# A hybrid attention and gating layer on eight cores: ordering by a build-time list scheduler, weights in column blocks, a lagging out-projection

## Chip, cores, metric

One Trainium2 chip, all 8 cores, each with one of the eight sequences of the batch and its own copy of the weights; nothing passes between cores. The metric is the device time of the slowest core in microseconds (us).

The program has a second, slower state: in some executions the cores of one die show a lower granted TensorE clock and take longer. Such runs are marked slow, and all ratios below are of fast runs only.

Names: PE is TensorE, DVE VectorE, ACT ScalarE, POOL GpSimd, SP the engine that issues most DMAs. SBUF is the memory in which the kernel keeps its tiles; its matmuls write to PSUM, here eight banks of 512 columns, which ScalarE or VectorE instructions then empty. A supertile is 512 rows of x (four tiles of 128); a sequence has eight.

In the profile lines, xn is the scaled x, xT its transpose, PT the exponentials of the scores, LR the attention gate over the softmax denominator, mixT the input of the out-projection, vln the layer norm of v_s and st_lr its scale, xe the copy of x for the residual, and pb or pp a PSUM bank.

## The reference, cut to what matters

```python
h = rmsnorm(x, norm_g)                                   # x: (8, 4096, 1024) float32
q, k, v, z_a, u, v_s, z_s = split(h @ w_in + b_in)       # 512,128,128,512,512,512,512 columns
attn = banded_sink_attention(q, k, v, sinks) * silu(z_a) # window 128, 8 heads of 64, 2 kv heads
u, v_s = gelu(u), gelu(v_s)
sgu = u * (tril(W_s) @ layernorm(v_s) + b_s) * silu(z_s) # in chunks of 128 positions
x = x + concat(attn, sgu) @ w_out + b_out                # residual, and a bias
return rmsnorm(x, final_norm_g)
```

## The kernel before: the parts that matter

Every engine runs a fixed list of instructions; semaphores are derived from declared reads and writes. PSUM banks are given out in rotation, whether the next one is free or not:

```python
def newbank():
    b = bank_ctr[0] % NB          # NB = 8
    bank_ctr[0] += 1
    return b
```

The weights arrive as three column ranges of eight row blocks, so the first projection needs all eight blocks of its range. The q and k groups are emptied by VectorE, and one set of two groups is issued as one piece of work:

```python
PIECES = [(0, 768), (768, 1792), (1792, 2816)]
# ... in fm_unit, after 8 matmuls for each group:
if func == AF.Identity:           # q and k
    S.op("dve", lambda e, ...: e.tensor_scalar(out=dst, in0=pbank[b][:], scalar1=bias_fm[:, fi:fi + 1], ...))
else:                             # gelu and silu groups
    S.op("act", lambda e, ...: e.activation(out=dst, in_=pbank[b][:], func=func, bias=...))
```

The bias b_out is added to x on GpSimd, at a fixed place in its list, before the residual needs it; x stays in SBUF from load to residual:

```python
def XB_units(st):                 # one per tile
    S.op("pool", lambda e: e.tensor_tensor(out=xs, in0=xs, in1=bout[:], op=ALU.add), ...)
```

The order of one supertile is written by hand (C1: scores, exp, masks; C2: values and denominators; Eu: out-projection of the same supertile; f: one projection piece of the next):

```python
f(1); C1_unit(st, 0)(); f(1); C1_unit(st, 1)(); C2_unit(st, 0)(); f(1)
C1_unit(st, 2)(); C2_unit(st, 1)(); Eu[0]()
f(1); C1_unit(st, 3)(); C2_unit(st, 2)(); Eu[1]()
f(1); C2_unit(st, 3)(); Eu[2](); f(100); Eu[3]()
# ... then XB_units, gelu groups, v_s, silu groups, mixing of the next supertile
```

The softmax here doesn't subtract the row's maximum and nothing guards it: scores larger than these inputs give would overflow.

## Time and profile before

| | before |
|---|---|
| times known at the prediction | 642.26, 643.53, 693.18 us |
| span of the profiled run, clock of its cores | 628.8 us, 0.949 to 0.959 |
| first attention scores | 89.3 us (the prediction reads 88.3) |
| seven periods from there | 492.0 us, 70.3 each |
| rest | 47.5 us |

A period here is the time from the first scores of one supertile to those of the next.

### The profile page before, as it was taken

To read this page: it belongs to the slowest core of one execution; us is meant where nothing else is said; L and a number is where in the kernel's file an instruction comes from. 1 tells how busy PE (TensorE), PEld (TensorE's weight loads), DVE (VectorE), ACT (ScalarE), POOL (GpSimd) and SP (SyncE) were. 2 spreads that over 40 slices of the span, in tenths; PEclk is the share of its full clock that TensorE was granted. 3 is DMA by queue.
4 is the path that set the end of the run, shared out by engine and by line. 5 is a ranking of instruction groups with operands and counts; after the bars stand their busy time and mean duration, and the time that the engine had idled before them with its cause. 6 is when DMAs were issued, how large, how long until landed. Compare 5 with 4: busy or idle time off the path is not lost.

```text
span 628.8 us, 9475 instructions; the slowest of 8 cores (623.3 to 628.8 us)
## 1 busy us (share of the span) xinstructions
PE 533.3 (85%) x3042; PEld 240.1 (38%) x3042; DVE 300.5 (48%) x510; ACT 346.6 (55%) x691; POOL 269.9 (43%) x286
## 2 busy tenths in 40 slices
PE   1569479899889998899889989899889989999673
PEld 1234233354434453344334443444335443444121
DVE  1230384445554464545545454545545454555244
ACT  4003573546853596557743695448734695443742
POOL 0464593274435353365336253456327253443310
PEclk9979787899999999999989999999989999999688
DMA  8999900240013200330013100340014100110002
GB/s 226 274 321 317 144 2 1 101 167 2 0 68 108 95 1 0 135 135 0 2 68 133 68 1 11 124 135 1 1 68 160 42 2 1 68 67 1 1 35 100
DMA packets 15747, 50.08 MB, mean 80 GB/s; under 512 B 2513, under 2 KB 2769, under 8 KB 15698
## 3 DMA queue, kind: packets, MB, share of 16 engines
q1 hardware_dynamic: 14546, 47.38, 22.5%
q0 software_dynamic: 1152, 2.10, 2.4%
q8 instruction: 25, 0.41, 0.3%
q14 instruction: 24, 0.20, 0.1%
HBM read 34.79 MB, written 16.78 MB: 82 GB/s over the span
## 4 chain that ended last, share of the span: by engine, by line
PE 49%; ACT 14%; issue 12%; DVE 9%; POOL 7%; DMA 7%; SPq 1%; POOLq 0%; DVEq 0%; ACTq 0%
PE pb L373 24%; PE pb L570 14%; DMA y_t<-w_in 7%; PE pb L422 5%; ACT PT L469 4%; DVE y_t L578 2%; ACT junk L584 2%; PE pb L401 2%; ACT LR L511 2%; POOL LR L516 2%; DVE st_bn L428 2%; POOL st_rs L314 2%; POOL st_lr L432 2%; PE pb L496 1%; DVE PT L478 1%
## 5 line engine op out<-in xcount | busy, mean ns | idle before, releaser
L373 PE MATMUL pb<-xT,w_in_bf 128*128 128x512 bf16 x1088 | 250.6, 388 | 11.8 <-POOL w_in_bf L266 8.5
L373 PEld LDWEIGHTS pb<-xT,w_in_bf 128*128 128x128 bf16 x1088 | 106.6, 100 | 147.5 <-issue 29.7
L570 PE MATMUL pb<-w_out_bf,mixT 128*128 128x512 bf16 x512 | 126.8, 405 | 22.2 <-DVE qT L379 16.5
L584 ACT ACTIVATE junk<-y_t 128x1024 bf16<-128x1024 f32 x32 | 33.8, 1057 | 124.4 <-DVE y_t L578 124.4
L474 POOL TENSOR_SCALAR_AFFINE_SELECT PT<-PT 128x512 bf16<-128x512 bf16 x62 | 42.6, 710 | 106.2 <-ACT PT L469 106.0
L570 PEld LDWEIGHTS pb<-w_out_bf,mixT 128*128 128x128 bf16 x512 | 50.6, 103 | 95.0 <-issue 48.4
L337 POOL TENSOR_TENSOR x_t<-x_t,bout_sb 128x1024 f32<-128x1024 f32 x32 | 82.4, 2607 | 0.0
L516 POOL TENSOR_TENSOR LR<-LR,zaT 128x512 f32<-128x512 f32 x32 | 36.9, 1154 | 105.8 <-ACT LR L515 105.8
L469 ACT ACTIVATE PT<-pb 128x512 bf16<-128x512 f32 x126 | 64.0, 606 | 18.7 <-PE pb L461 18.6
L422 PE MATMUL pb<-w_in_bf,xT 128*128 128x512 bf16 x256 | 60.7, 380 | 0.0
L432 POOL TENSOR_TENSOR st_lr<-st_ve,neghalf 128x1 f32<-128x1 f32 x32 | 17.6, 551 | 88.5 <-DVE st_ve L430 88.5
L593 DVE SCALAR_TENSOR_TENSOR y_t<-y_t,st_fr,gf_sb 128x1024 f32<-128x1024 f32 x32 | 44.6, 1394 | 23.0 <-ACT st_fr L591 23.0
L520 DVE TENSOR_TENSOR mixT<-pb,LR 128x512 bf16<-128x512 f32 x32 | 22.1, 692 | 67.9 <-POOL LR L516 64.9
L578 DVE TENSOR_TENSOR y_t<-pb,x_t 128x512 f32<-128x512 f32 x64 | 41.0, 681 | 15.3 <-PE pb L570 15.3
L426 ACT ACTIVATE vs_f<-pb 128x512 f32<-128x512 f32 x32 | 19.1, 597 | 52.2 <-PE pb L424 26.1
L478 DVE TENSOR_TENSOR PT<-PT,mask_sb 128x512 bf16<-128x512 bf16 x64 | 30.7, 514 | 25.8 <-ACT PT L469 25.8
L543 POOL TENSOR_TENSOR gate<-uT,zsT 128x512 bf16<-128x512 bf16 x32 | 39.6, 1268 | 1.8 <-ACT zsT L383 1.8
L428 DVE BATCH_NORM_STATS2 st_bn<-vs_f 128x6 f32<-128x512 f32 x32 | 22.0, 688 | 36.4 <-ACT vs_f L426 36.4
L511 ACT ACTIVATE LR<-pb,esink_col 128x128 f32<-128x128 f32 x128 | 37.1, 389 | 3.2 <-PE pb L501 3.2
L434 DVE TENSOR_SCALAR vln<-vs_f,st_mv,st_lr 128x512 bf16<-128x512 f32 x32 | 17.5, 546 | 37.4 <-POOL st_lr L432 37.4
L305 ACT ACTIVATE junk<-x_t 128x1024 bf16<-128x1024 f32 x32 | 33.7, 1054 | 1.9
L496 PE MATMUL pb<-PT,v_r 128*64 128x512 bf16 x126 | 20.9, 407 | 16.2 <-DVE PT L478 13.4
(59 smaller groups left out, 536.4 us busy)
## 6 DMA issues: line engine op xcount, KB each, us to landing
x_t<-x SPq DMA_DIRECT2D x32, 512.0 KB, 4.0
out<-y_t SPq DMA_DIRECT2D x32, 512.0 KB, 2.8
x_t<-w_in SPq DMA_DIRECT2D x10, 512.0 KB, 9.0
y_t<-w_in SPq DMA_DIRECT2D x6, 512.0 KB, 10.1
x_t<-w_in SPq DMA_DIRECT2D x6, 384.0 KB, 9.2
w_out_bf<-w_out POOLq DMA_DIRECT2D x8, 256.0 KB, 9.3
y_t<-w_in SPq DMA_DIRECT2D x2, 384.0 KB, 11.5
sgt<-sgu_wT SPq DMA_DIRECT2D x1, 512.0 KB, 7.1
```

Source lines behind the costliest of these rows:

```text
L337: S.op("pool", lambda e: e.tensor_tensor(out=xs, in0=xs, in1=bout[:], op=ALU.add), reads=[("x", slot), "c_bout"], writes=[("x", slot)])
L373: ins = e.matmul(pbank[b][:], lhsT=w_in[:, k, col:col + 128], rhs=xT[:, k, :], start=(k == 0), stop=(k == 7))
L422: e.matmul(pbank[b][:], lhsT=xT[:, k, tt * 128:(tt + 1) * 128], rhs=w_in[:, k, OFF_VS:OFF_VS + 512], start=(k == 0), stop=False)
L469: S.op("act", lambda e, g=g, kb=kb, b=b: e.activation(out=PT[:, pp, kb, g, :], in_=pbank[b][:], func=AF.Exp, scale=0.125), reads=[("pb", b ...
L474: return e.affine_select(out=v, in_=v, pattern=[[0, 4], [-1, 128]], compare_op=ALU.is_ge, fill=0.0, base=-1, channel_multiplier=1)
L511: ins = e.activation(out=LR[:, lb, c * 128:(c + 1) * 128], in_=pbank[bd_][:, c * 128:(c + 1) * 128], func=AF.Ln, bias=esink_col[:, c:c + 1])
L516: S.op("pool", lambda e: e.tensor_tensor(out=LR[:, lb, :].rearrange("p (c q) -> p c q", c=4), in0=LR[:, lb, :].rearrange("p (c q) -> p c q ...
L543: S.op("pool", lambda e, jj=jj, gb=gb: e.tensor_tensor(out=gate[:, gb, :], in0=uT[:, jj, :], in1=zsT[:, jj, :], op=ALU.mult), reads=[("uT" ...
L570: ins = e.matmul(pbank[banks[hf]][:], lhsT=mixT[:, ec, tt * 128:(tt + 1) * 128], rhs=w_out[:, ec, hf * 512:(hf + 1) * 512], start=(ec == 0 ...
L578: ins = e.tensor_tensor(out=y_t[:, ys, hf * 512:(hf + 1) * 512], in0=pbank[banks[hf]][:], in1=x_t[:, slot, hf * 512:(hf + 1) * 512], op=AL ...
L584: S.op("act", lambda e: e.activation(out=junk[:], in_=y_t[:, ys, :], func=AF.Square, accum_out=st_fs[:, ys:ys + 1]), reads=[("y", ys)], wr ...
L593: S.op("dve", lambda e: e.scalar_tensor_tensor(out=y_t[:, ys, :], in0=y_t[:, ys, :], scalar=st_fr[:, ys:ys + 1], in1=gf[:], op0=ALU.mult, ...
```

## The change

The hand-written order is replaced by a graph of operations with estimated costs and a list scheduler that runs at build time. At each step it takes the operation that can start first on any engine, and it gives a PSUM bank to whatever starts next. Some operations may go to either of two engines. Otherwise:

- weights in 22 column blocks of 128 (each enough for one group of eight matmuls);
- the out-projection of a supertile is offered one supertile later (the lag), so it can fill TensorE during attention;
- x is loaded a second time for the residual, and GpSimd adds b_out to this copy;
- one exp and one mask over two banks (1024 columns), and powers on GpSimd in place of small Ln and Exp.

The diff has 1,400 lines; its core is this (cuts marked):

```diff
-def newbank(): ... rotation ...
-run(A_pre_units(0)) ... f(1); C1_unit(st, 0)(); ...          # order by hand
+class Scheduler:                                             # cut to the choice
+    while done < len(ops):
+        for e in ENGS:
+            for o in avail[e]:
+                est = max(free[e], o.nready)                 # and the earliest free bank
+                # skip if another allowed engine would finish earlier by estimate
+                key = (est, o.prio, o.n)
+        ... take the best, free[e] = est + cost ...
+# weights
+def load_w(cb): G.op("sp", dma w_in[cb] ...); G.op({"dve": (1.22, fn), "pool": (2.6, fn)}, ...)
+# either engine
+G.op({"act": (1.16, fa), "dve": (0.85, fd)}, ...)            # xn: scaling of x
+G.op({"dve": (0.68, copy), "act": (1.06, copy)}, ...)        # xT out of PSUM
+G.op({"dve": (0.745, ...), "act": (0.69, ...)}, ...)         # q, k out of PSUM
+G.op({"dve": (0.75, mul), "pool": (1.25, aff)}, ...)         # mask of 1024 columns
+# second read of x, bias
+def load_xe(n):
+    G.op("sp", dma xe <- x[n] ...)
+    G.op("pool", lambda e: e.tensor_tensor(out=xe[:, s, :], in0=xe[:, s, :], in1=bout[:], op=ALU.add), cost=2.6, ...)
+# lag: out_tile(4 * (st - 1) + tt) is offered together with attention(st, j)
```

## The prediction

> **What bounds the kernel now.** I looked first at the cores and the granted clock, then at the page's busy line and 40 slices, then at the order of TensorE's work in one supertile of 512 rows, its waits, and the chain that ended last. From the page of the kernel before:
>
> ```profile
> PE 533.3 (85%) x3042; PEld 240.1 (38%) x3042; DVE 300.5 (48%) x510; ACT 346.6 (55%) x691; POOL 269.9 (43%) x286
> ...
> PE   1569479899889998899889989899889989999673
> ...
> PEclk9979787899999999999989999999989999999688
> DMA  8999900240013200330013100340014100110002
> GB/s 226 274 321 317 144 2 1 101 167 2 0 68 108 95 1 0 135 135 0 2 68 133 68 1 11 124 135 1 1 68 160 42 2 1 68 67 1 1 35 100
> ```
>
> TensorE is the only engine near its limit, and not everywhere: slices 0 to 4 (0 to 79 us) are a start-up in which the DMA is full and TensorE is not; then comes a plateau; the last two slices fall off. The timeline gives the boundaries. The first attention scores start near 88.3 us, the same point of the eighth supertile is at 581.3 us, so seven periods take 493.0 us (70.4 each); the last attention and out-projection take 47.5 us more.
>
> How short could a period be? I take start-to-start times from the timeline at full clock: 32 projection matmuls 6.90 us (0.216 each), 16 of the out-projection 3.46, the four v_s tiles 8.59, the V block 1.79, 16 transposes 0.99, four scores 0.54, one attention tile's eight value and denominator matmuls 0.98, the mixing 1.0. A supertile has 136, 64, 1, 1, 32, 16, 4 tiles and 1 of these: 29.3 + 13.8 + 8.6 + 1.8 + 2.0 + 2.1 + 3.9 + 1.0 = **62.5 us**, so 8 x 62.5 = 500 us for the program. The span of 628.8 us has 129 us in which the array does not stream at full rate. TensorE's waits between 131 and 551 us (six periods) show why:
>
> ```profile
> PE pb L570 <- DVE qT L379: 14.0, 11, 2.3
> PE pb L461 <- ACT PT L469: 8.6, 6, 1.4
> PE pb L496 <- DVE PT L478: 6.1, 6, 1.0
> PE pb L373 <- ACT zsT L383: 2.2, 6, 0.4
> ```
>
> They sum to some 32 us with the small ones, 5.3 per period. The out-projection does not need qT: it waits for the bank that the fixed rotation gives it, until VectorE, behind other work in its fixed order, has emptied a q projection from it. The timeline shows that such a pause costs twice:
>
> ```profile
> 322.69 0.60 PE L501 MATMUL pb<-PT,ones 128*64 128x512 bf16 x4
> 325.29 5.30 PE L570 MATMUL pb<-w_out_bf,mixT 128*128 128x512 bf16 x16 [2.00 <-DVE qT L379]
> ...
> 338.49 3.62 PE L570 MATMUL pb<-w_out_bf,mixT 128*128 128x512 bf16 x16
> ```
>
> After 2.00 us of idleness the same 16 matmuls take 1.7 us longer; in that stretch the granted clock is 0.77, 0.50, then 0.70. This happens in every second period (70.7 against 69.0 us).
>
> **What the Trainium skill says.** "TensorE: Matmul & The Clock Gate", Part 1: an idle array falls to half clock and needs a few us of work to return; the window is free-running. The trace agrees (0.50 above), and shows that a 2.0 us pause can be enough. The same part says that dense matmuls on three or more cores of a die take it to a 13/16 clock. This profile does not show that: the seven periods ran at 0.98. Of the three times, 693.18 us may be such a state, but has no trace. "PSUM — Partial Sum Buffer", Specifications: eight banks, and GpSimdE reads none of them; in the trace every pb tile is read by ACT or DVE, so only they can empty banks for the new scheduler. "DMA: Bandwidth & Descriptors", Queues, rings and completion order: each DMA engine takes turns between the rows that have work. So w_out on GpSimd's queue will share the engines with weights still in flight on SyncE's. Before it ran after them (144 GB/s in slice 4, engines full), so no row shows the sharing yet.
>
> **The change, part by part.** The matmuls are the same, 3042 on both sides, so 500 us remains the floor for TensorE; what can shrink is the 129 us beside it.
>
> Steady state. Banks go to whichever group is next instead of in rotation; q, k, xn and xT may be emptied by ACT or DVE (in the built order 20 of 40 q and k groups and 9 of 32 transposes go to ACT); the out-projection of the supertile before fills TensorE while attention waits for ACT. In the built order the attention phase has out groups between scores and values. Other engines per period: exp over two banks instead of one (63 instead of 126 of 606 ns) and no tiny Ln and Exp of the final norm (64 of 204 ns) relieve ACT, which takes some q and xT copies instead; it stays near the 43.5 us it has now. DVE gets 57 double masks (at most 2 x 514 ns) for 64 single ones, gives up 12 q and k groups (745 ns), 9 xT copies (683), and takes 19 more x scalings (852): near 38 against 36. GpSimd loses 56 of 62 masks (710 ns) and gains 32 pairs of small operations (190 + 551 ns) for the final norm: 82.4 + 39.6 + 36.9 us of unchanged rows and about 75 us of small ones, 29 per period. All are far below 62.5. I leave 2 us per period for waits and changes of array tiling, no re-warming: 64.5 against 70.4, times seven: **-41 us**.
>
> Start. Before: 88.3 us until the first scores. After: weights come in column blocks, and each of 22 blocks lets one group of eight matmuls run, so TensorE follows the DMA. What must land before the V block, last in the order, on SyncE's queue: 4 tiles of x, 22 blocks, two late constants, 4 tiles of the next x, 3 of the one after (the built order puts these between the blocks), 35 x 0.524 = 18.3 MB, with 1.2 MB of constants on ACT's queue. Slices 0 to 3 delivered 3.55 MB by 15.7 us, then about 0.318 MB per us. Block 15 (26 transfers, 14.8 MB with constants) lands near 53 us, the V block (19.6 MB) near 66 us. But w_out is released block by block from block 14 on; alone it took 2.1 MB at about 0.135 MB per us, about 2 us each; six of them before the V block push it to **about 78 us**. By then TensorE has done two sets of transposes, twelve u and gate groups, v_s, mixing, five q and k groups, two of the next supertile and a few scores: 47 us. Left: 500 - 47 = 453. Before, at 88.3 us, some 44 were done and 455 left. So the start gains about **-10 us**: much less than "weights arrive by column" promises, as the same bytes must come and more x is put before them.
>
> End. Before: 47.5 us for 19.7 us of matmuls. After, the out-projections of the last two supertiles (27.6 us) and attention (6 us) are left together; they cover the last softmax chain, perhaps 4 us of gaps remain, and about 8.5 us after the last matmul (residual, square, power, scale, store) are as before. **-15 us**.
>
> x twice. 16.8 MB more reads: at plateau the DMA share is 0.16 and 56 GB/s flow; one period's 4 more tiles (2.1 MB) take 7 us of DMA in 64. Hidden.
>
> Sum: 79.5 (V block landed, converted, copied) + 453 + 7 x 2 + 4 + 8.5 = 559 us of span. Before, the median of 643.53 is 14.7 above the profile's span; added: **573 us**. By differences: 643.5 - 41 - 10 - 15 = 577; I choose 571 between them and a slightly luckier DMA order.
>
> **Rivals.** (1) A new wait replaces the old: the order on every engine is fixed at build time from estimated costs, and a strict order of gelu, silu and exp phases on ACT forbids matmuls of a later phase. If semaphore delays, or ACT in the attention phase (four tiles of 2 x 1.04 + 1.17 + 0.63 us plus eight squares of 1.25: 26 us beside 32 us of matmuls), slip, 4 to 5 us per period stay, and the time is 590 to 600. For it: ACT is tight there. Against: the costs in the source (0.69, 1.25, 2.6, 1.73 us) match the trace's rows (691, 1054 + 189, 2607, 8 x 216 ns). (2) The start stays DMA-bound: w_out and early x push the V block to 85 us: 580. If the engines overlap both queues better than I assume, it lands at 68: 561. (3) The denser array trips the 13/16 clock in every run: 500/0.8125 = 615 us of matmuls, about 660 to 670 in all, slower. Against: the plateau is 92% busy now without it. Chance 3%.
>
> **Range and chances.** The start varies by 10 us either way, the bubbles by 10, the end by 3: low 549, high 593. Faster by over 2% is below 630.7 us, which only rival 3 or a badly wrong order misses.
>
> **What would show it.** Right: TensorE at 9 from slice 6 to nearly the end, periods of 64 to 65 us, no wait on a bank above 5 us in total, clock near 0.99 after the start, DMA at 9 until about 80 us, HBM reads of about 51 MB. Wrong: exp or a mask as TensorE's largest wait on the plateau (rival 1), projections waiting for weights beyond 80 us (rival 2), clock near 0.81 on all cores (rival 3).

## More of the kernel before

The prediction shows the page, the waits and the timeline. What it did not look at closely is the following view, the groups of instructions of VectorE and GpSimd by shape. After the count come the busy time in us and the mean of one in ns, then the idle time before the group and who ended it.

```profile
L478 DVE TENSOR_TENSOR PT<-PT,mask_sb 128x512 bf16<-128x512 bf16 x64 | 30.7, 514 | 25.8 <-ACT PT L469 25.8
...
L434 DVE TENSOR_SCALAR vln<-vs_f,st_mv,st_lr 128x512 bf16<-128x512 f32 x32 | 17.5, 546 | 37.4 <-POOL st_lr L432 37.4
```

The first is a mask on the exponentials, the second the output of the layer norm of v_s (vln); both are means over the whole run. The prediction took such means for fixed costs. The layer norm comes close to one (544 to 548 ns), the mask does not: half of them take 426 ns or less, the longest 2559.

## The result, and the profile after

| | before | after |
|---|---|---|
| median, all runs of the comparison | 642.89 us (4 runs) | 592.67 us (4 runs, all fast) |
| fastest run | 630.42 us | 591.43 us |
| ratio of fast runs | | 0.9404 (0.9373 to 0.9435) |

A ratio is the mean time of one kernel's fast runs over that of the other's of the same rounds, so it is not quite the ratio of the medians quoted. The gain looks larger in the medians because the three times known before were all slow runs: the fourth took 630.42 us, and in later rounds the fast runs of the kernel before lay between 625.75 and 630.71. In the terms of those rounds (about 628 us) the changed kernel takes **590.6 us**; the runs below are compared with that. As the ratio rests on one fast run of the kernel before, its interval is 2 us either way, and every gain below carries that. The kernel is 6% faster, and 21.7 us slower than predicted.

The mean granted clock of a die rose. Before:

```profile
die 0 (median of its cores): 623.7 us, clock 0.953
```

After:

```profile
die 0 (median of its cores): 587.4 us, clock 0.984
```

Most of this lies at the two ends (0.89 to 0.96 until the first scores, 0.76 to 0.93 from the last supertile's first scores on, on the profiled core); in the six periods between, it rose from 0.99 to 1.00, as the half-clock stretches are gone.

The page of the changed kernel, to be read against the page in the prediction:

```profile
PE 523.7 (89%) x3042; PEld 233.3 (39%) x3042; DVE 346.1 (59%) x438; ACT 331.0 (56%) x566; POOL 251.4 (43%) x277
...
PE   0688696999999899999899889999999889989971
...
PEclk9999988999999899999999999999999999999997
DMA  8999980510135312132213105230421013200342
...
HBM read 51.57 MB, written 16.78 MB: 116 GB/s over the span
```

TensorE is at 9 or near it from slice 7 on, but there are 8s on the whole plateau: this is where the time is missing. TensorE's waits for a named releaser (us in all, times, longest) show what took the place of the waits before:

```profile
PE pp L481 <- DVE xn L467: 14.6, 4, 12.2
PE pp L577 <- DVE vln L552: 8.0, 5, 2.7
PE pp L497 <- DVE w_fm L447: 7.5, 4, 4.7
PE pp L634 <- DVE mixT L657: 4.2, 4, 1.7
PE pp L681 <- DVE mixT L657: 3.7, 3, 1.8
PE pp L634 <- DVE v_r L526: 3.4, 1, 3.4
```

The first and third belong to the start. The others are waits for VectorE, of two kinds. L577 waits for the layer norm, its input. L634 has PT and v_r as inputs, not mixT: where it waits for mixT, it waits for a PSUM bank that VectorE has yet to empty. With the smaller waits of that kind (L681 for xe and xT, L481 for xT, L497 for xe) some 8 us of bank waits are left after the first scores. I add up the timeline of TensorE from first scores to first scores, and subtract from each period its number of matmuls at full-clock durations. This gives the loss of each period:

| part of the span (us) | predicted | measured |
|---|---|---|
| until the first scores | 79.5 | 81.25 |
| matmuls at full rate after that | 453 | 452.6 |
| losses in eight supertiles | 7 x 2 + 4 = 18 | 8.6, 8.2, 2.2, 7.4, 3.8, 5.0, 5.2, 4.6 = **45.0** |
| after the last matmul | 8.5 | 12.5 |
| span | 559 | 591.3 |

The split between the second and third row depends a little on the durations that are called full-clock (with those of the prediction it is 455.5 and 42.1); differences between runs of the same order do not. So the losses are what went wrong. Why is VectorE late? Its groups by shape, changed kernel:

```profile
L625 DVE TENSOR_TENSOR PT<-PT,mask_sb 128x1024 bf16<-128x1024 bf16 x57 | 57.0, 1012 | 5.5 <-ACT PT L612 4.7
...
L686 DVE TENSOR_TENSOR xe<-pp,xe 128x512 f32<-128x512 f32 x64 | 43.6, 686 | 55.3 <-PE pp L681 48.6 <-POOL xe L667 6.5
L552 DVE TENSOR_SCALAR vln<-vs_f,st_mv,st_lr 128x512 bf16<-128x512 f32 x32 | 27.4, 857 | 22.9 <-POOL st_lr L550 22.4
...
L467 DVE TENSOR_SCALAR xn<-xa,st_rs 128x1024 bf16<-128x1024 f32 x23 | 20.8, 918 | 16.9 <-POOL st_rs L461 11.9 <-PE pp L481 4.9
```

The layer-norm output has the same shape as before and takes 857 ns instead of 546. The residual (L686), which reads PSUM, takes 686 ns where it took 681. A mean hides how this comes about. Here is the timeline of VectorE in one stretch, then that of GpSimd (start, duration, instruction):

```profile
230.97 1.60 DVE L625 TENSOR_TENSOR PT<-PT,mask_sb 128x1024 bf16<-128x1024 bf16 x1
232.49 0.74 DVE L503 TENSOR_SCALAR qT<-pp,bias_fm_sb 128x512 bf16<-128x512 f32 x1
233.15 0.68 DVE L657 TENSOR_TENSOR mixT<-pp,LR 128x512 bf16<-128x512 f32 x1
233.75 1.57 DVE L625 TENSOR_TENSOR PT<-PT,mask_sb 128x1024 bf16<-128x1024 bf16 x1
```

```profile
230.87 1.16 POOL L653 TENSOR_TENSOR LR<-LR,zaT 128x512 f32<-128x512 f32 x1 [4.60 <-ACT LR L651]
231.98 2.80 POOL L667 TENSOR_TENSOR xe<-xe,bout_sb 128x1024 f32<-128x1024 f32 x1
```

A mask with GpSimd idle takes 0.68 or 0.69 us (33 of 33 in this run). The first mask here begins 0.10 us after GpSimd's LR product, which ends at 232.03, and ends at 232.57, 0.54 us later: it stood still until GpSimd was done. Now the bias addition, which was issued while the mask worked, takes 2.80 us instead of 2.35: it stood still in turn. The q and mixT instructions, which read PSUM, run beside it in 0.74 and 0.68 us, undisturbed. The second mask begins at 233.75 inside the bias addition and ends at 235.32, 0.54 us after the addition (234.78). So it is in the whole run: 18 masks began inside an LR product or a bias addition, and each ended 0.55 us after it.

The Trainium skill describes this: "SBUF — State Buffer", section "SBUF: two separate sides", says that VectorE and GpSimd share a pair of SBUF ports under an exclusive lock, which GpSimd contends for with VectorE instructions in a two-port mode or (where GpSimd reads SBUF) with two SBUF inputs; who starts first holds it for the whole instruction and the other blocks. The trace agrees with it in both directions, with the numbers above. The prediction had not looked it up.

This is a mechanism, not yet the cause of the missing time. The experiments ask whether these collisions cost TensorE the 27 us of losses, or whether the order, the estimates or the second read do.

### The profile page after: what moved, and what is told of

The parts are those of the page before. It is cut to its first block, busy times and chain, and to the rows that moved or that the text cites. A ratio compares the mean times of both kernels' runs of the same rounds, so it can differ in the third digit from the quotient of the medians.

```text
span 591.3 us, 9383 instructions; the slowest of 8 cores (586.4 to 591.3 us)
## 1 busy us (share of the span) xinstructions
PE 523.7 (89%) x3042; PEld 233.3 (39%) x3042; DVE 346.1 (59%) x438; ACT 331.0 (56%) x566; POOL 251.4 (43%) x277
## 3 DMA queue, kind: packets, MB, share of 16 engines
q0 software_dynamic: 1152, 2.10, 2.2%
## 4 chain that ended last, share of the span: by engine, by line
PE 62%; DVE 9%; issue 9%; ACT 6%; POOL 6%; DMA 6%; SPq 0%; POOLq 0%; DVEq 0%; ACTq 0%
PE pp L497 29%; PE pp L681 14%; PE pp L537 6%; DMA xe<-w_in 4%; PE pp L634 2%; PE pp L607 2%; PE pp L522 2%; DVE vln L552 2%; PE pp L638 2%; DMA xa<-x 2%; PE pp L481 2%; POOL st_lr L550 1%; ACT LR L647 1%; DVE st_bn L543 1%; PE pp L577 1%
## 5 line engine op out<-in xcount | busy, mean ns | idle before, releaser
L497 PE MATMUL pp<-xT,w_fm 128*128 128x512 bf16 x1088 | 249.9, 387 | 10.1 <-DVE w_fm L447 7.5
L497 PEld LDWEIGHTS pp<-xT,w_fm 128*128 128x128 bf16 x1088 | 104.9, 99 | 146.5 <-issue 30.8
L681 PE MATMUL pp<-w_out_bf,mixT 128*128 128x512 bf16 x512 | 119.8, 380 | 6.3 <-DVE mixT L657 3.7
L667 POOL TENSOR_TENSOR xe<-xe,bout_sb 128x1024 f32<-128x1024 f32 x32 | 78.8, 2466 | 24.4 <-DMA xe<-x 21.6
L686 DVE TENSOR_TENSOR xe<-pp,xe 128x512 f32<-128x512 f32 x64 | 43.6, 686 | 55.3 <-PE pp L681 48.6
L681 PEld LDWEIGHTS pp<-w_out_bf,mixT 128*128 128x128 bf16 x512 | 46.2, 98 | 67.9 <-issue 20.2
L695 DVE SCALAR_TENSOR_TENSOR xe<-xe,st_fr,gf_sb 128x1024 f32<-128x1024 f32 x32 | 51.3, 1603 | 23.8 <-POOL st_fr L693 21.5
L612 ACT ACTIVATE PT<-pp 128x1024 bf16<-128x1024 f32 x63 | 62.7, 1032 | 0.2 <-PE pp L607 0.2
L537 PE MATMUL pp<-w_vs,xT 128*128 128x512 bf16 x256 | 60.7, 380 | 0.9 <-ACT uT L507 0.9
L625 DVE TENSOR_TENSOR PT<-PT,mask_sb 128x1024 bf16<-128x1024 bf16 x57 | 57.0, 1012 | 5.5 <-ACT PT L612 4.7
L541 ACT ACTIVATE vs_f<-pp 128x512 f32<-128x512 f32 x32 | 19.1, 596 | 40.7 <-PE pp L538 16.7
```

Source lines behind the costliest of these rows:

```text
L497: ins = e.matmul(bank(h), lhsT=w_fm[:, cb, k, :], rhs=xT[:, xb, k, :], start=(k == 0), stop=(k == 7))
L537: e.matmul(bank(h), lhsT=xT[:, xb, k, tt * 128:(tt + 1) * 128], rhs=w_vs[:, k, :], start=(k == 0), stop=False)
L612: G.op("act", lambda e, h=h, kb=kb: e.activation(out=PT[:, p2, kb, :], in_=bank2(h), func=AF.Exp, scale=0.125), uses=[h], writes=[("PT", p ...
L625: return e.tensor_tensor(out=v, in0=v, in1=mask[:, kb, :].unsqueeze(1).to_broadcast([128, 2, 512]), op=ALU.mult)
L667: G.op("pool", lambda e: e.tensor_tensor(out=xe[:, s, :], in0=xe[:, s, :], in1=bout[:], op=ALU.add), reads=["c_bout"], writes=[("xe", s, 0 ...
L681: ins = e.matmul(bank(h), lhsT=mixT[:, mb, ec, tt * 128:(tt + 1) * 128], rhs=w_out[:, ec, hf * 512:(hf + 1) * 512], start=(ec == 0), stop= ...
```

## Experiments

All give the reference's result unless said otherwise. "us" is the median of all runs of an experiment; the ratio is of fast runs, to those of the kernel before in the same rounds. A gain in us is a difference of ratios times 628; gains of 2 us (e1_dma_order, e11_reread_tiny) are not clear of the interval of 0.9404.

| run | edit to the changed kernel | us | ratio (95%) |
|---|---|---|---|
| (changed kernel) | | 592.67 | 0.9404 |
| e9_bias_tiny | bias addition one column, same order | 568.58 | 0.9062 (0.9047-0.9078) |
| e10_bias_single | bias addition as two one-input instructions, same order | 572.99 | 0.9135 (0.9119-0.9151) |
| e11_reread_tiny | second read 16 columns, same order | 588.23 | 0.9376 (0.9353-0.9400) |
| e2_bias_dve | bias addition on VectorE | 572.25 | 0.9115 (0.9091-0.9139) |
| e3_recost | scheduler's costs from the trace | 583.05 | 0.9276 (0.9249-0.9303) |
| e4_tail_xa | no second read in the last supertile | 586.74 | 0.9328 (0.9295-0.9362) |
| e1_dma_order | weights before everything else | 589.22 | 0.9375 (0.9350-0.9401) |
| e5_fix_evac | xn on ACT; q, k, xT on DVE | 575.74 | 0.9167 (0.9141-0.9194) |
| e16_xn_act | xn on ACT alone | 574.51 | 0.9137 (0.9093-0.9180) |
| e17_q_dve | q, k, xT on DVE alone | 586.00 | 0.9326 (0.9297-0.9354) |
| e6_no_lag | no lag | 605.78 | 0.9632 (0.9588-0.9675) |
| e7_rot_banks | banks in rotation | 638.96 (one fast run: 600.14) | none |
| e12_best1 | e5 + e2 + e4 | 568.22 | 0.9058 (0.9040-0.9076) |
| e13_best2 | e12 + e1 | 571.35 | 0.9094 (0.9060-0.9127) |
| e15_best1_gate | e12 + gate product on DVE | 570.61 | 0.9078 (0.9041-0.9115) |
| e8_before_q_act | *kernel before*, q and k on ACT | 637.29 | 1.0152 (1.0128-1.0176) |
| e14_before_bias_tiny | *kernel before*, bias addition one column | 623.18 | 0.9914 (0.9883-0.9944) |

### The collision, with the order held fixed

The theory: VectorE blocked by GpSimd's bias addition makes TensorE wait. The rivals: a poor order, or the second read. Most edits make the scheduler choose another order, and then two things change at once. In the next three runs the estimated cost is left alone and only the executed instruction is changed, so TensorE, VectorE and ScalarE run the same instructions in the same order as the changed kernel.

**One column instead of 1024** (b_out is missing for the other columns; with its small values the result stays within tolerance):

```diff
-    G.op("pool", lambda e: e.tensor_tensor(out=xe[:, s, :], in0=xe[:, s, :], in1=bout[:], op=ALU.add), cost=2.6, ...)
+    G.op("pool", lambda e: e.tensor_tensor(out=xe[:, s, 0:1], in0=xe[:, s, 0:1], in1=bout[:, 0:1], op=ALU.add), cost=2.6, ...)
```

> The changed kernel with GpSimd's bias addition cut to one column, its estimated cost left at 2.6 us, so that the order on every engine is unchanged (result wrong on purpose: b_out is missing). Theory A (while GpSimd runs this two-input addition, VectorE's instructions on SBUF operands are stretched, come later than planned, and TensorE waits for them): masks fall from a mean of 1012 ns to 700 to 800, the layer-norm output from 857 to below 650, and the time by 12 to 20 us to 570 to 578 (ratio to before 0.91 to 0.921). Theory B (the order itself is poor, durations matter little): less than 5 us, ratio above 0.932.

Measured: 568.58 us, 0.9062, some 22 us below the changed kernel (0.9404 - 0.9062 = 0.0342, times 628): theory A, and slightly more than it said. Groups of VectorE in this run:

```profile
L625 DVE TENSOR_TENSOR PT<-PT,mask_sb 128x1024 bf16<-128x1024 bf16 x57 | 45.6, 808 | 7.5 <-ACT PT L612 6.5
...
L552 DVE TENSOR_SCALAR vln<-vs_f,st_mv,st_lr 128x512 bf16<-128x512 f32 x32 | 22.4, 699 | 17.1 <-POOL st_lr L550 16.6
```

Masks fell from 1012 to 808 ns and the layer norm from 857 to 699, each a little less than expected, as other GpSimd instructions still collide. Because the order is the same, the losses compare period by period: 8.6, 8.2, 2.2, 7.4, 3.8, 5.0, 5.2, 4.6 became 3.2, 1.8, 2.1, 2.5, 3.7, 2.9, 3.9, 4.6, **45.0 to 24.7 us**, with 1.8 us at the start and 1.9 after the last matmul on top. TensorE's wait for the layer norm went from 8.0 to 0.9 us. So with nothing else changed on the three engines, this one instruction costs 22 us.

The cut also frees GpSimd itself, so there is a second way: what stands behind the addition in GpSimd's own list comes earlier. As the orders are equal, the two traces can be compared matmul by matmul to see where the changed kernel falls behind. After the first scores there are seven such places of 1 us or more. At six of them VectorE was held: masks of 2.83 us (TensorE waits at 91.9 us) and 2.54 (280.9), the final scaling of 3.48 (171.8), layer norms of 2.09 (330.1 and 463.3) and 2.49 (530.6). At the seventh, and second largest, it was GpSimd's list:

```profile
195.82 2.36 POOL L667 TENSOR_TENSOR xe<-xe,bout_sb 128x1024 f32<-128x1024 f32 x1 [2.50 <-DVE st_mv L545]
198.26 0.46 POOL L547 TENSOR_SCALAR st_ve<-st_mv 128x1 f32<-128x1 f32 x2
```

The input of the last st_ve was ready at 195.80, but behind the addition st_ve could begin only at 198.26; the layer norm came as much later, and TensorE waited 2.7 us at 201.55. So some 3 of the 20 us of losses are GpSimd's own lateness and not the lock; the smaller places (0.4 to 0.8 us each) I have not traced one by one.

**The control: two instructions with one input each**

```diff
-    e.tensor_tensor(out=xe[:, s, :], in0=xe[:, s, :], in1=bout[:], op=ALU.add)
+    e.tensor_scalar(out=junkp[:], in0=bout[:, 0:512], scalar1=1.0, scalar2=0.0, ...)
+    e.tensor_scalar(out=xe[:, s, :], in0=xe[:, s, :], scalar1=1.0, scalar2=0.0, ...)
```

> Control for the last run: the bias addition is replaced by two GpSimd instructions with one tensor input each (a copy of 512 elements and a multiplication of 1024 by 1.0), some 1.7 us together instead of 2.47; order unchanged on TensorE, VectorE and ScalarE (result wrong on purpose). Theory A1 (it is the second input of GpSimd's instruction that collides with VectorE): masks and layer-norm outputs as short as with the one-column addition, 700 to 800 and below 650 ns, and most of its gain. Theory A2 (any large GpSimd instruction collides, or it is GpSimd's occupancy that delays its own small instructions, st_ve and st_lr): masks stay above 900 ns and half of the gain or less.

Measured: 572.99 us, 0.9135, most of the gain; masks 904 ns and layer norm 758, between the two runs. Neither rival came out as written. The timeline of VectorE and then of GpSimd shows why:

```profile
84.09 1.50 DVE L625 TENSOR_TENSOR PT<-PT,mask_sb 128x1024 bf16<-128x1024 bf16 x1
```

```profile
84.02 1.04 POOL L667 TENSOR_SCALAR xe<-xe 128x1024 f32<-128x1024 f32 x1
```

A one-input instruction blocks the mask just as well: it ends 0.53 us after GpSimd does. What differs is how long a holder keeps the other out: the addition holds for 2.35 us, the longer of these for about 1 us, and VectorE can get in between the two. So the second input is not the point. GpSimd's time for the two is also less in all (60.3 us for 78.8), so this run does not tell the length of one instruction from their sum.

**The second read, 16 columns instead of 1024** (result wrong)

```diff
-    dma_start(out=xe[:, s, :], in_=x_d[n * 128:(n + 1) * 128, :])
+    dma_start(out=xe[:, s, 0:16], in_=x_d[n * 128:(n + 1) * 128, 0:16])
```

> The changed kernel in which the second read of x brings 16 columns instead of 1024; same instructions in the same order on every engine (result wrong on purpose). Theory A (the second read is hidden except at the end, where the last tiles' read, bias addition and residual stand in a row): 3 to 6 us less than 590, all of it after the last attention, ratio 0.930 to 0.936. Theory B (the reads delay GpSimd, which waits 21.6 us for them in its fixed order, and with it the layer norm): 8 us or more, with the losses within the periods down from 42 us.

Measured: 588.23 us, 0.9376: 0.3% or 2 us, below what either theory expected and not clear of the noise of the comparison. GpSimd's wait for these reads fell from 21.6 to 6.5 us and TensorE got nothing for it. The prediction's "Hidden" for reading x twice holds for the traffic.

**The addition on VectorE**, as one would really mend it:

```diff
-    G.op("pool", lambda e: e.tensor_tensor(out=xe..., in0=xe..., in1=bout[:], op=ALU.add), cost=2.6, ...)
+    G.op("dve",  lambda e: e.tensor_tensor(out=xe..., in0=xe..., in1=bout[:], op=ALU.add), cost=1.22, ...)
```

> One edit to the changed kernel: the addition of b_out to x (32 x 2466 ns) moves from GpSimd to VectorE. Theory 'VectorE is stretched by GpSimd's two-input operations': the mask's mean falls from 1012 to below 800 ns, vln's from 857 to below 650, TensorE's waits for vln and mixT after the start fall from 16 us to below 8, and the time falls by 6 to 12 us although VectorE has 39 us more work. Rival 'the order on the engines is wrong whatever the durations' : the waits stay and the time is within 3 us, or rises by VectorE's new work.

Measured: 572.25 us, 0.9115: 18 us below the changed kernel, although VectorE got 40 us more work (32 x 1269 ns). The wait for the layer norm fell from 8.0 to 0.2 us, those for mixT rose from 7.9 to 10.5. Giving more work to the engine that was late made the kernel faster, though the order changed too.

**True costs for the scheduler** (mask 0.75 to 1.01 us, layer norm 0.55 to 0.86, final scaling 1.39 to 1.60, delay from another engine to TensorE 0.10 to 0.27, and small ones):

```diff
-    G.op({"dve": (0.75, mul), "pool": (1.25, aff)}, ...)
+    G.op({"dve": (1.01, mul), "pool": (1.54, aff)}, ...)
```

> One edit to the changed kernel: the scheduler's costs are set to the mean durations of the changed kernel's trace (mask 1.01 for 0.75, vln 0.86 for 0.55, final scale 1.60 for 1.39, and so on) and the delay into TensorE from 0.10 to 0.27 us. Theory 'wrong costs make a wrong order': TensorE's waits for vln, mixT and banks after the start (some 22 us) halve, time down by 6 to 12 us. Rival 'contention': means are right only on average, single operations still last 0.7 or 2.8 us, and the time changes by less than 4 us.

Measured: 583.05 us, 0.9276, 8 us. Better estimates recover about a third. A likely reason, not tested, is that the plan leaves room for the average delay, while a delay comes as 1 to 2 us in one place and none in another.

**Was the collision there before?** The same cut to one column in the kernel before:

```diff
-    S.op("pool", lambda e: e.tensor_tensor(out=xs, in0=xs, in1=bout[:], op=ALU.add), ...)
+    S.op("pool", lambda e: e.tensor_tensor(out=xs[:, 0:1], in0=xs[:, 0:1], in1=bout[:, 0:1], op=ALU.add), ...)
```

> The kernel before with the same addition on GpSimd cut to one column, all orders fixed as they are (result wrong on purpose). In the kernel before, the mean durations of VectorE's masks (514 ns for 512 columns) and layer-norm outputs (546 ns) show few collisions. Theory A (the list scheduler moved the addition beside VectorE's work, the loss is new in the changed kernel): within 6 us of 628, ratio 0.99 to 1.0. Theory B (the loss was there before as well and the change only kept it): 15 us or more, ratio below 0.976.

Measured: 623.18 us, 0.9914, 5 us. The kernel before paid 5 us for its 82 us of bias additions, the changed one 22 for 79. About 17 us of it are new: the scheduler places the additions without knowing that they collide.

### The choice of engine

```diff
-    G.op({"act": (1.16, fa), "dve": (0.85, fd)}, ...)                     # xn
+    G.op({"dve": (0.85, fd)} if st == 0 else {"act": (1.16, fa)}, ...)    # xn
-    G.op({"dve": (0.68, ...), "act": (1.06, ...)}, ...)                   # xT
+    G.op({"dve": (0.68, ...)}, ...)
-    G.op({"dve": (0.745, ...), "act": (0.69, ...)}, ...)                  # q, k
+    G.op({"dve": (0.745, ...)}, ...)
```

> The changed kernel with the choice of engine taken back: q, k and xT groups emptied by VectorE alone, x scaled by ScalarE after the first supertile, as before; banks still dynamic. Theory A (what was gained is the freedom to order and to take any free bank; VectorE at 346 us of 591 has room for 20 x 0.745 + 9 x 0.68 us more): within 6 us of the changed kernel's 590, so ratio to before 0.935 to 0.95. Theory B (the two-way choice of engine is what took the bank waits away): VectorE waits on a bank come back at 2 us per period, and the ratio goes to 0.965 to 0.985.

Measured: 575.74 us, 0.9167. Both theories fell: taking the choice back makes it 15 us *faster* and brings no bank waits back. The periods after the first are 64.3, 65.3, 64.3, 64.3, 64.6 and 64.0 us: the 64.5 of the prediction. Two further runs divide it, xn alone and the rest alone:

> Half of the run in which evacuations were fixed (575.7, 15 us below the changed kernel): only the scaling of x goes to ScalarE after the first supertile; q, k and xT keep their choice of engine. Theory A (the scaling reads x from SBUF and is stretched beside GpSimd, 918 ns on average and 749 ns undisturbed; taking it off VectorE is what helped): 572 to 580, ratio 0.912 to 0.924. Theory B (fixing q, k and xT helped, or only another order fell out): 584 or more, ratio 0.930 and up.

> The other half: q, k and xT are emptied by VectorE alone (reads of PSUM, never seen stretched: 0.68 and 0.75 us whatever GpSimd does), the scaling of x keeps its choice. Theory A: no gain, VectorE has more work beside the stretched scalings: 586 to 598, ratio 0.933 to 0.953. Theory B: most of the 15 us, 574 to 582.

Measured: 574.51 us (0.9137) for xn alone, and 586.00 (0.9326) for q, k and xT alone, a gain of 5 us, just below what theory A allowed (no gain). The groups of VectorE with xn on ScalarE:

```profile
L625 DVE TENSOR_TENSOR PT<-PT,mask_sb 128x1024 bf16<-128x1024 bf16 x55 | 49.1, 903 | 6.6 <-ACT PT L612 5.8
...
L467 DVE TENSOR_SCALAR xn<-xa,st_rs 128x1024 bf16<-128x1024 f32 x4 | 2.9, 751 | 12.0 <-POOL st_rs L461 12.0
```

The scaling reads and writes SBUF, is blocked like the masks (918 ns on average on VectorE, 751 undisturbed) and pushes what stands behind it; on ScalarE it takes 1147 ns on average (1135 to 1152 for the nine in the changed kernel). The scheduler saw 0.85 against 1.16 us and chose VectorE where that finished earlier. The order changes with this edit too, so how much of the 15 us is collision and how much order is not settled by these runs.

### The parts that were meant to gain

**Without the lag** (the out-projection follows its own attention; the priorities of the out-projection, the second read and the bias addition move with it):

```diff
-    if st > 0: out_tile(4 * (st - 1) + tt)   # before attention(st, j)
+    out_tile(4 * st + tt)                    # after attention(st, j)
```

> The changed kernel without the lag: the out-projection of a supertile follows its own attention, as before; everything else stays. Theory A (the lagging out-projection is what fills TensorE while the softmax chain of ScalarE and the masks run): TensorE waits for masks or for mixT in every period, 2 to 5 us each, and the time goes up by 15 to 35 us (ratio 0.965 to 1.0). Theory B (the projections of the next supertile are filling enough): within 8 us of 590.

Measured: 605.78 us, 0.9632, so the lag is worth some 14 us: theory A, just below its range. The periods become 66.8 to 71.7 us. TensorE's waits between 147 and 530 us:

```profile
PE pp L607 <- DVE sgt L585: 10.8, 5, 2.2
PE pp L607 <- ACT PT L612: 4.2, 8, 0.8
PE pp L634 <- ACT PT L612: 3.1, 6, 0.5
```

Waits of the scores (L607) for a bank and of the values (L634) for exp come back, which the lagging out-projection had covered.

**Banks in rotation, the scheduler knowing it:**

```diff
+    only = next bank in turn, for groups of class "P"
+    if only is not None and i != only: continue
```

> The changed kernel with its projection groups (transposes, projections, mixing, out-projection) forced to take banks in a fixed rotation, the list scheduler still choosing the order knowing that. Theory A (with an order that knows the rotation, a dynamic choice adds little): 0 to 8 us more than 590, ratio 0.94 to 0.953. Theory B (dynamic banks carry the gain): bank waits of TensorE above 10 us in all and a ratio of 0.965 or more.

Measured: correct, but three of four runs were slow (638, 640, 686 us; in the last, one die at a clock of 0.81 throughout), so there is one fast run, 600.14 us, and no ratio. In its profile the periods are 65.2, 64.0, 66.4, 63.9, 66.4 and 64.0 us, no longer than with dynamic banks (65.0, 60.9, 66.1, 67.7, 65.4, 67.4). One group waits 19.1 us for its turn in the start and the first scores come at 91.9 us instead of 81.25, but this is made up: the second supertile's come at 147.3, against 147.9. What is longer is the end: 45.8 us from the eighth supertile's first scores to the last matmul, against 38.4, with one wait of 5.0 us for mixT, and 15.7 us after it, against 12.5. On time this run is inconclusive. On the plateau dynamic banks show no gain in this one run, but its order also collides less (masks take 802 ns on average), so the two effects are not separated.

**One part alone in the kernel before: q and k emptied by ScalarE**

```diff
-    S.op("dve", lambda e, ...: e.tensor_scalar(out=dst, in0=pbank[b][:], scalar1=bias_fm[:, fi:fi + 1], ...))
+    S.op("act", lambda e, ...: e.activation(out=dst, in_=pbank[b][:], func=AF.Identity, bias=bias_fm[:, fi:fi + 1]))
```

> One part of the change done alone on the kernel before: q and k groups are emptied by ScalarE instead of VectorE; nothing else moves. Theory A (the wait of the out-projection for the q bank on VectorE, 14.0 us in six periods, and the half-clock stretches after it, about 1.7 us in every second period, are what the steady state loses): the wait goes, and the time falls by 12 to 25 us from 628 (ratio 0.96 to 0.98). Theory B (ScalarE's fixed order then makes the same bank wait, behind exp): a wait on ScalarE takes its place, within 8 us of 628 or slower.

Measured: 637.29 us, 1.0152: 1.5% slower, theory B. TensorE's waits in the stretch that the prediction shows for the kernel before (131 to 551 us):

```profile
PE pb L570 <- ACT qT L379: 9.9, 6, 1.7
PE pb L570 <- DVE mixT L520: 9.5, 5, 2.1
PE pb L461 <- ACT PT L469: 8.6, 6, 1.4
```

The 14.0 us for VectorE's qT became 9.9 us for ScalarE's qT and 9.5 for mixT, which ScalarE's later softmax probably delays. In this fixed order, moving the named releaser only moved the wait.

Not varied alone were the column blocks of the weights, the exp and mask over two banks, and the powers on GpSimd.

### The start and the end

**Weights first**: x of the second supertile only after block 12, that of the third, w_out and the late constants after the last weights.

```diff
-    reads=[("w", 14 + k)], writes=[("w_out", k)]
+    reads=[("w", 21)],     writes=[("w_out", k)]
+    # load_xa: reads=[("w", 12)] if st == 1 else [("w", 21)] if st == 2 else []
```

> One edit to the changed kernel: the next tiles of x wait until weight block 12 (the ones after: block 21) has been converted, b_out, the final gain and w_out wait for blocks 18 to 21, so that nothing but the weights is in the queue ahead of them. Theory 'the start is bound by bytes ahead of the weights': 14.8 MB instead of about 20 MB stand before the V block, it lands near 55 us instead of 77, the first attention value matmul moves from 91.9 us to about 75 to 80, and the time falls by 8 to 14 us to about 580. Rival 'the start is bound by TensorE's own 47 us of work and the cold clock': below 4 us.

Measured: 589.22 us, 0.9375, 2 us. The V block was converted at 64 us instead of 77, so its lateness really was bytes ahead of it in the DMA (w_out, late constants and early x, moved together). But the time did not follow. The timeline of TensorE, then of VectorE, then of GpSimd shows where it stood next:

```profile
82.43 1.01 PE L481 MATMUL pp<-ident_sb,xn 128*128 128x128 bf16 x8 [5.71 <-DVE xn L467]
86.84 1.86 PE L481 MATMUL pp<-ident_sb,xn 128*128 128x128 bf16 x16 [3.40 <-DVE xn L467]
```

```profile
79.52 2.76 DVE L467 TENSOR_SCALAR xn<-xa,st_rs 128x1024 bf16<-128x1024 f32 x1 [0.18 <-POOL st_rs L461]
...
83.76 2.83 DVE L467 TENSOR_SCALAR xn<-xa,st_rs 128x1024 bf16<-128x1024 f32 x1
```

```profile
79.39 2.33 POOL L667 TENSOR_TENSOR xe<-xe,bout_sb 128x1024 f32<-128x1024 f32 x1
...
83.25 5.54 POOL L667 TENSOR_TENSOR xe<-xe,bout_sb 128x1024 f32<-128x1024 f32 x2
```

TensorE waits 9.1 us for the scaled x of the second supertile, and two of its scalings take 2.8 us behind bias additions. I took this for the reason and tested it below (e13_best2).

**No second read at the end.** In the last supertile xa still holds x, so the residual can take it from there:

```diff
+    xr = xa if st == NS - 1 else xe      # and no dma into xe for the last four tiles
```

> One edit to the changed kernel: the last supertile's residual is taken from xa, which nothing overwrites any more, instead of being read a second time into xe. Theory 'the second read is on the path at the end': the 12.5 us between the last matmul and the end fall to about 8.5, time down by 3 to 5 us. Rival 'hidden, as predicted': within 1 us.

Measured: 586.74 us, 0.9328, about 5 us. The chain that ended last in the changed kernel has what it removes:

```profile
574.79 5.24 DMA xe<-x
580.17 2.34 POOL xe L667
```

The last read of x was issued at 574.79, as it stood behind stores in one queue and needed a buffer that a store had to free; the last residual could begin only at 582.67, 3.9 us after TensorE's last matmul (578.76). The 12.5 us after the last matmul, against 8.5 predicted, are these 4 us.

### Together

> Three mends together: q, k and xT emptied by VectorE and x scaled by ScalarE (575 alone), bias addition on VectorE (572 alone), no second read for the last supertile (586.7 alone against 590). If they mend different losses: 560 to 566, ratio 0.893 to 0.902. If the first two mend the same loss (VectorE late beside GpSimd's additions): 566 to 573, ratio 0.902 to 0.913.

The three mends (x scaled on ScalarE and q, k, xT on VectorE; bias addition on VectorE; no last second read) give 568.22 us, 0.9058 to the kernel before and 0.963 to the changed kernel (0.9058 / 0.9404), correct: the best correct version here. Alone they gained 15, 18 and 5 us; together 22. So the first two mend the same loss for the most part, as the second case of the expectation has it. All losses are now 2.4 to 3.1 us per period, except 7.6 at the end. The edit is the sum of those shown.

> The three mends of the last run (568.2 us, ratio 0.906) and the weights ahead of w_out, the late constants and the early x. Alone that order brought the V block 13 us earlier and the time only 1 to 2 us down, as TensorE then waited for the scaled x of the second supertile behind stretched VectorE work. Theory A (the start's gain was eaten by the same contention, which is gone here): 558 to 564 us, ratio 0.889 to 0.899. Theory B (the bytes that are put behind the weights are needed just as soon): 565 to 570, ratio 0.901 to 0.909.

Weights first in this version: 571.35 us, 0.9094, no gain, though GpSimd's additions are gone. My reading of e1_dma_order was wrong, or at most part of it. The timeline of TensorE in this run:

```profile
81.76 1.01 PE L481 MATMUL pp<-ident_sb,xn 128*128 128x128 bf16 x8 [4.16 <-ACT xn L466]
83.72 1.01 PE L481 MATMUL pp<-ident_sb,xn 128*128 128x128 bf16 x8 [0.95 <-ACT xn L466]
```

The first scores come at 66.0 us, yet the transposes of the second supertile still come at 81.8, now behind ScalarE. Its x was not the reason: the last of it landed at 57.6 us (42.3 in e12_best1) and was squared by 62.6. What came late was the power on GpSimd that gives its scale, st_rs:

```profile
63.12 1.16 POOL L588 TENSOR_TENSOR mixT<-sgt,uT 128x512 bf16<-128x512 f32 x1 [5.77 <-DVE w_v L447]
...
78.43 1.84 POOL L461 TENSOR_TENSOR st_rs<-st_ms,neghalf 128x4 f32<-128x4 f32 x1
```

GpSimd's list first waits until 63.12 for the last weight block, which was staged in mixT; then three products, eight issues of w_out and four masks stand before the power. In e1_dma_order the same power began at 78.37, in e12_best1 at 45.9. So this edit moved the delay from the DMA to GpSimd's list, and what an earlier V block would be worth without that was not run.

> The three mends and the product of u and its gate on VectorE (0.4 us estimated) instead of GpSimd (1.21 us), beside which layer-norm outputs took 1.30 us instead of 0.55. Theory A (each collision that is left costs TensorE something): 2 to 5 us below the 568.2 of the three mends, ratio 0.897 to 0.903. Theory B (what is left of collisions is off TensorE's path; its losses are 2.4 us per period of changes of array tiling, and the ends): within 2 us, ratio 0.903 to 0.909.

The gate product on VectorE too (edit: "pool" to "dve", cost 1.27 to 0.40): 570.61 us, 0.9078, the same within the interval. So taking this collision away brings nothing: theory B.

## Why the prediction was right or wrong, point by point

- **TensorE's floor and its place as the bound: right.** 452.6 us of streaming after the first scores, 453 predicted.
- **Steady state, "I leave 2 us per period for waits and changes of array tiling": this is the step that failed.** With 4 at the end it was 18 us; 45.0 were measured. It rests on "All are far below 62.5", and the sum behind that came true: in the six periods between the first scores of the second and the eighth supertile VectorE was busy 38.3 us per period, 35.9 before ("near 38 against 36"). What failed is the step from that sum to few waits. Durations of the kernel before were taken for constants: the mask's 1012 ns on average are within the "at most 2 x 514 ns", but single ones took 0.68 to 2.84 us, layer norms 0.53 to 2.49, and TensorE stood behind the long ones. With the order unchanged and the bias addition cut, the losses are 24.7 and the time is 22 us lower, which is the size of the miss. What is left over the 18, some 7 us, I have not traced to one cause; mixT waits of 1.7 us, one of them in each of two late periods, are most of what is listed.
- **Bank waits and half-clock pauses go: right for the most part.** Some 8 us of bank waits are left after the first scores, against 25 in six periods before (14.0 + 8.6 + 2.2 and a small one). No named one is above the 5 us of the prediction's sign (4.2 for mixT is the largest), their sum is. The clock in the six periods is 1.00.
- **Rival 1, "a new wait replaces the old": it happened, at its 590 to 600, by another way.** It expected semaphore delays or ScalarE, and the prediction held against it that the costs in the source "match the trace's rows". They did match the rows of the kernel before. It was held to be unlikely on the very ground that fails when two engines share ports.
- **Start, the V block at "about 78 us": right** (converted at 77 to 78.5; first scores 81.25 for 79.5). That bytes ahead of it set this is shown by e1_dma_order, not which of them. Rival 2 is not closed: 13 us earlier gave 2, but that edit held up GpSimd's list instead.
- **End: tail 8.5 predicted, 12.5 measured.** "As before" overlooked that the second read stands in that chain; e4_tail_xa gives 5 us back. This is the one place where the second read was seen not to be hidden.
- **"The median of 643.53 is 14.7 above the profile's span; added": wrong.** That median is a slow run; fast runs are 1.5 us above the span. This error of 13 us went the other way: the span was missed by 32 us (559 against 591.3), the time only by 22. That the time came out nearer is luck.
- **Rival 3, the lower clock in every run: did not come.** A clock near 0.81 was seen on one die in single runs: of the kernel before (692.84 us) and of variants of the changed one (657.11, 686.26).
- **Two readings are off, without weight for the result.** 88.3 us is where transposes before the first scores start; the scores start at 89.3. And 3.55 MB by 15.7 us is what slice 0 alone delivered; slices 1 to 3 average 0.304 MB per us, not 0.318.

## What to carry to other kernels

Before summing durations for a new order, ask for each pair of engines that will now run side by side whether they share ports, and look at the shortest and longest duration of one instruction, not only the mean: 0.69 and 2.8 us for the same mask say what 1.01 hides. That an engine's busy time adds up to far less than the period does not say that nobody waits for it. To test whether an instruction's collisions cost time, shorten what is executed and leave the order alone, and compare the two traces instruction by instruction, as the engine that you relieve comes earlier too; an edit that makes a scheduler choose again changes two things at once. A scheduler that may choose between engines by duration needs to know what that choice collides with, or it is better fixed: here instructions that read SBUF belonged off VectorE, or GpSimd's long ones off GpSimd.

## What the Trainium skill lacked or had wrong

- "SBUF — State Buffer": the lock is described and agrees (a mask of 0.69 us stretched to 2.8, a GpSimd addition of 2.35 us to 2.80). That GpSimd's holder keeps the lock "for the whole instruction" does not hold for its very small ones: four layer-norm outputs that lay wholly inside power instructions of 128 x 4 elements (1.0 to 1.8 us long by the profile, whose spans on GpSimd are rough) took 0.53 to 0.55 us, as when alone. What the page lacks is what the lock costs in a kernel: 22 of 590 us, for 79 us of bias additions.
- "TensorE: Matmul & The Clock Gate", Part 1, has the 13/16 clock come with dense matmuls on three cores of a die. Here all eight cores ran the same dense program in every run; the cores of fast ones held a mean clock of 0.94 to 1.00, and 0.81 on all cores of one die was seen in single executions (686.26 us with banks in rotation), so the load alone does not bring it.
- No page has a measured case in which an instruction is better placed on the slower engine because of this lock: a scaled copy of x (SBUF to SBUF, 128 x 1024) takes 0.75 us on VectorE and 1.15 us on ScalarE, and moving it to ScalarE gained 17 us (e16_xn_act; a new order is part of it).
